# An indexer moved from split products on the whole array to plain float32 products on quarters of its rows

## The chip, the cores and the metric

The kernel runs on one core of a Trainium2 chip. The metric is device time in microseconds (us), the median of the timed runs. TensorE's granted clock stands at its upper level, 2.4 GHz, in every slice of the profile.

## What is computed

The reference is a trunk of two layers over 256 tokens of 1024 channels. Each layer projects the normed input to queries, keys and values of two attentions and to the inputs of a small "indexer"; the indexer's scores choose, for each query, the 64 keys that the first attention may look at. Then come both attentions, an output product and a gated feed-forward block. The change touches the indexer alone:

```python
iq = apply_rope(iq.reshape(b_, s_len, IDX_HEADS, IDX_DIM), cos_i, sin_i)   # 8 heads of 32
ik = apply_rope(ik[:, :, None, :], cos_i, sin_i)[:, :, 0, :]               # one key of 32
...
dots = jnp.einsum('bqhd,bsd->bqhs', iqb, ik, preferred_element_type=jnp.float32) * (IDX_DIM ** -0.5)
w = iwb.astype(jnp.float32) * (IDX_HEADS ** -0.5)
score = jnp.einsum('bqhs,bqh->bqs', jax.nn.relu(dots), w)
score = jnp.where(admissible[None], score, -jnp.inf)
_, idx = lax.top_k(score, topk)
```

## The kernel before, in words

The 256 tokens are two blocks (b = 0, 1) of 128, one per partition. All weights stream once from HBM in chunks of about 1 MB (`load`, L157). Each chunk is split in two halves: ScalarE casts it to `whi` (type float32r) at L174, VectorE writes the rest, `wlo`, at L175. A large product is then three matmuls, hi·hi, lo·hi and hi·lo (`mm3`, L193 to L198), each 512 columns wide as a rule. The main stream of TensorE takes the projections of a layer in the order idx, qb, kb, vb, qa, ka, va, then the output product (`wo`), gate and up (`ps_gate`, `ps_up`) and down (`dn`).

Between the large products stand small ones, as "threads": transposes, the indexer's products (`dots`), the logits (`lg_b`, `lg_a`) and so on. The class `Weave` sets TensorE's order when the program is built: a thread yields an estimated delay or names of events, `W.spend` adds an estimated cost to a running clock, and a thread goes on as soon as that clock has passed its due time. `DIX` is the delay between an indexer projection and its transposes, `DG` that between groups of two heads of the indexer. So TensorE's order is fixed by hand; ScalarE and VectorE are ordered by the framework's scheduler. Each engine executes its list in order, and a waiting instruction holds up all that stand behind it.

The indexer, for a block: the projection lands in `ps_idx`; `rope_evac` (L365) copies it to SBUF and rotates it, and L390 adds the two parts to `ixt`, nine vectors of 32 per token (eight queries, one key). L392 to L398 split these in hi and lo and lay them side by side, (hi, lo, hi, lo) for a query and (hi, hi, lo, lo) for the key, so that one head fills all 128 rows of the array and a single matmul of type float32r does all four products. L404 to L411 transpose the nine 128x128 squares (`ptx`, L202) and copy them to `iqT` and `ikT`. In `indexer` (L435) the eight heads come in four groups of two: two matmuls (L446) into one PSUM bank, a relu by ScalarE (L448), and two multiply-adds by VectorE (L451) into `score`. After that VectorE searches the 64 largest.

There are eight PSUM banks. A projection holds two of them while it accumulates; each `ptx`, `ptq` (transposes of the other queries and keys) and each group of `dots` takes one and gives it back when ScalarE has read it. `relu` has two buffers.

A plain float32 matmul of the program shows as two records in the trace, each with its own weight load; a float32r matmul and a transpose show as one.

Of the kernel before, what the change touches and what calls it, by code (L numbers as in the profile page):

```python
# [8 lines left out]
F32 = mybir.dt.float32  # L9
# [8 lines left out]
P = 128  # L18
# [14 lines left out]
LOWP = 100  # L33
DG = 2.0
DUP = 2.5
# [6 lines left out]
DROPE = 8.0  # L42
DIX = 13.0
DB = (8.0, 10.0)
# [4 lines left out]
class Weave:  # L49
    """Orders the tensor engine's work: one main stream of large products, and threads of small  # L50
    ones, each of which says how long (in estimated microseconds) its operands take to be ready."""

# [56 lines left out]
def tile_hybrid_trunk(ctx, tc, x, w_in, w_out, vecs, w_gate, w_up, w_down, g_final, rope, out):  # L109
# [5 lines left out]
    def bank(name):  # L115
        return psum.tile([P, 512], F32, tag="bank", bufs=8, name=name)
# [3 lines left out]

    # ---------------------------------------------------------------- weight stream
    NSUB = 1024
# [78 lines left out]
    def transpose(o, i):  # L201
        nc.tensor.transpose(o, i, ident)  # L202
        W.spend(0.107)

    # ---------------------------------------------------------------- inputs that stay
    LAMROW = 2 * DEPTH * KT + DEPTH
# [28 lines left out]

    # gains and lambda vectors, one per column
    gT = pool.tile([P, ROWS], F32, tag="gT", name="gT")
# [57 lines left out]
    def split_psum(pt, name, scales=None, tag="act", bufs=12):  # L295
        """Columns of a bank as hi and lo tiles; scales: one factor per partition for each of them."""
        n = pt.shape[1]
# [49 lines left out]
    def norm(kind, L, b, h):  # L347
        """One half of the transposes of x, scaled by the gain (the row factor is applied to the products)."""
        yield DN, ()
        norm_T(kind, L, b, h)  # L350
        norm_split(kind, L, b, h)
        if h == 1:
            rstd[kind, L, b] = norm_rstd(b, f"{kind}{L}{b}")

    # ---------------------------------------------------------------- what follows a projection
    T = {}

    def matT(t, o, name):
        """[tokens, 512] -> [128, 4, tokens], float32."""
        pt = bank(f"ptq_{name}").rearrange("p (k t) -> p k t", k=4)  # L360
        for k in range(4):
            transpose(pt[:, k], t[:, k * P:(k + 1) * P])
        nc.scalar.copy(o, pt)
# [17 lines left out]
    def after_proj(L, nm, b, ps):  # L381
        name = f"{nm}{L}{b}"
        r = rstd["mix", L, b]
        if nm == "idx":
# [3 lines left out]
            a, c = rope_evac(ps, r, b, 9, 32, name)  # L388
            t = pool.tile([P, 9, 32], F32, tag="hff", bufs=3, name=f"ixt{L}{b}")
            nc.vector.tensor_tensor(t.rearrange("p h d -> p (h d)"), a[:, :288], c[:, :288], op=ALU.add)  # L390
            # hi and lo side by side: (hi, lo, hi, lo) of a query meets (hi, hi, lo, lo) of a key
            sq = pool.tile([P, 8, 4, 32], F32R, tag=("kbT", "kaT")[b], bufs=1, name=f"ixq{L}{b}")  # L392
            sk = pool.tile([P, 1, 4, 32], F32R, tag="ixk", bufs=2, name=f"ixk{L}{b}")
            for st, hd, first, second in ((sq, slice(0, 8), slice(0, 4, 2), slice(1, 4, 2)),
                                          (sk, slice(8, 9), slice(0, 2), slice(2, 4))):
                src = t[:, hd].unsqueeze(2).to_broadcast([P, hd.stop - hd.start, 2, 32])
                nc.scalar.copy(st[:, :, first], src)
                nc.vector.tensor_tensor(st[:, :, second], src, st[:, :, first].bitcast(F32), op=ALU.subtract)  # L398
            yield DIX, ()
            iq = pool.tile([P, 8, P], F32R, tag="iqT", bufs=2, name=f"iqT{L}{b}")  # L400
            if b == 0:
                T["ik"] = pool.tile([P, S], F32R, tag="ikT", bufs=1, name=f"ikT{L}")
            flat = [v.bitcast(F32).rearrange("p h r d -> p h (r d)") for v in (sq, sk)]
            for g in range(2):  # L404
                pt = bank(f"ptx{L}{b}{g}").rearrange("p (k t) -> p k t", k=4)
                for k in range(4):
                    transpose(pt[:, k], flat[0][:, 4 * g + k])
                nc.scalar.copy(iq[:, 4 * g:4 * g + 4], pt)
            pt = bank(f"ptx{L}{b}2")
            transpose(pt[:, :P], flat[1][:, 0])  # L410
            nc.scalar.copy(T["ik"][:, b * P:(b + 1) * P], pt[:, :P])  # L411
            T["iq", b] = iq
        elif nm in ("va", "vb"):
# [15 lines left out]

    # ---------------------------------------------------------------- attention  # L430
    def small_mm(cost, *a, **k):
        nc.tensor.matmul(*a, **k)  # L432
        W.spend(cost)

    def indexer(L):  # L435
        for b in range(NB):
            yield 0, tuple(("idx", L, i) for i in range(b + 1))
            nk = (b + 1) * P
            sc = pool.tile([P, S], F32, tag="score", bufs=2, name=f"score{L}{b}")
            first = True  # L440
            for g in range(4):
                if g:
                    yield DG, ()
                ps = bank(f"dots{L}{b}{g}").rearrange("p (i k) -> p i k", i=2)
                for i in range(2):
                    small_mm(0.109, ps[:, i, :nk], T["iq", b][:, 2 * g + i], T["ik"][:, :nk], start=True, stop=True)  # L446
                rl = pool.tile([P, 2, S], F32, tag="relu", bufs=2, name=f"relu{L}{b}{g}")
                nc.scalar.activation(rl[:, :, :nk], ps[:, :, :nk], AF.Relu, scale=32 ** -0.5)  # L448
                for i in range(2):
                    h = 2 * g + i  # L450
                    nc.vector.scalar_tensor_tensor(sc[:, :nk], rl[:, i, :nk], T["iw", b][:, h:h + 1],  # L451
                                                   smask[:, b, :nk] if first else sc[:, :nk],
                                                   op0=ALU.mult, op1=ALU.add)
                    first = False
# [12 lines left out]
    def softmax_pair(L, b, q, k, mask, pair, name):  # L467
        """Unnormalized probabilities of two heads of one row group, and one over their sums."""
        nk = (b + 1) * P
# [120 lines left out]

    # ---------------------------------------------------------------- the feed-forward block
    ffT = {}
# [15 lines left out]

    # ---------------------------------------------------------------- the main stream
    def group(kind, L, key, n, first, after):  # L610
        """act @ w for both blocks; first: the acts are only being made, so one block after the other."""
        banks = [bank(f"ps_{key[1]}{L}{key[2] if len(key) > 2 else ''}{b}") for b in range(NB)]
# [95 lines left out]
    def final(b, cuts, gfin):  # L708
        """The last norm of one block, piece by piece as its columns come."""
        n = len(cuts)  # L710
# [28 lines left out]
    def startup(after):  # L739
        n = NCOL["idx"]  # L740
        with tc.manual_schedule(engines={ENG.Activation, ENG.DVE}):
# [15 lines left out]

            # the first block in plain float32, which waits for no splitting
            first = [begin(0, h) for h in range(2)]
# [85 lines left out]
```

## Time and profile before

| | us |
|---|---|
| median of 3 runs | 647.33 (646.92 to 649.78) |
| profiled execution, span from first to last instruction | 645.0 |
| TensorE busy | 635.2 (98% of the span) |
| VectorE busy | 437.9 (68%) |
| ScalarE busy | 365.2 (57%) |

The profiled execution is known by its span alone; it lies 2.3 us under the median of the runs. Busy time of TensorE is that of its matmul records, whose ends are modelled, so a small wait can hide in it; the distance between the starts of two records tells more. An engine's idle time matters only where TensorE waits for it.

### The profile page before, as it was taken

Reading aid. Unit: us, or ns where it says so; the run is one execution under the profiler, and the core shown is the slowest. Engines: PE = TensorE matmul, PEld = TensorE weight load, DVE = VectorE, ACT = ScalarE, POOL = GpSimd, SP = SyncE. Lnnn points to the kernel's source line nnn. Section 1 sums busy time; section 2 is a strip of 40 time slices with the busy share of each in tenths; the row PEclk is TensorE's granted clock in tenths of the full one; section 3 lists DMA queues with packets and bytes.
Section 4 is the critical chain, followed back from the end, with each engine's and each line's share of the span. In section 5 each row is a group of like instructions: output and inputs, shape, how many; then the busy total and the mean of one; then the engine's idle time right before and its main releaser. Section 6 shows DMA issues by size and latency. Waiting matters only on the chain.

```text
span 645.0 us, 8819 instructions
## 1 busy us (share of the span) xinstructions
PE 635.2 (98%) x3256; PEld 526.5 (82%) x3256; DVE 437.9 (68%) x922; ACT 365.2 (57%) x636; POOL 1.9 (0%) x12
## 2 busy tenths in 40 slices
PE   8999999999999999999999999999999999999995
PEld 5888787888888889888898888778888888898885
DVE  6899997596456555544598999866765455464445
ACT  7868586675544454333487678765744554443322
POOL 1000000000000000000000000000000000000000
PEclk9999999999999999999999999999999999999999
DMA  9773453326555655555276533323655555555501
GB/s 317 228 227 101 133 187 136 131 90 236 188 168 170 197 193 196 175 191 162 69 262 203 188 131 132 132 65 131 215 180 193 195 196 166 197 163 193 196 34 65
DMA packets 49907, 108.59 MB, mean 168 GB/s; under 512 B 1826, under 2 KB 8520, under 8 KB 49864
## 3 DMA queue, kind: packets, MB, share of 16 engines
q1 hardware_dynamic: 49392, 106.96, 49.6%
q10 hardware_dynamic: 472, 1.07, 0.5%
q8 instruction: 25, 0.41, 0.3%
q14 instruction: 18, 0.15, 0.1%
HBM read 106.97 MB, written 1.05 MB: 167 GB/s over the span
## 4 chain that ended last, share of the span: by engine, by line
PE 97%; DMA 1%; DVE 0%; SPq 0%; ACT 0%; issue 0%; ACTq 0%
PE ps_gate L196 6%; PE ps_gate L198 6%; PE dn L196 6%; PE dn L197 6%; PE dn L198 6%; PE ps_gate L197 6%; PE ps_up L198 6%; PE ps_up L196 6%; PE ps_up L197 6%; PE wo L198 2%; PE wo L196 2%; PE wo L197 2%; PE lg_a L432 2%; PE pth L202 1%; PE ps_va L196 1%; PE ps_vb L196 1%
## 5 line engine op out<-in xcount | busy, mean ns | idle before, releaser
L175 DVE TENSOR_TENSOR wlo<-wraw,whi 128x1024 fp32r<-128x1024 f32 (+1 forms) x204 | 244.5, 1205 | 141.9 <-ACT whi L174 138.4
L174 ACT CAST whi<-wraw 128x1024 fp32r<-128x1024 f32 (+1 forms) x204 | 209.6, 1040 | 150.8 <-PE dn L197 50.0
L196 PE MATMUL ps_gate<-whi,hi_ffn 128*128 128x512 f32 (+1 forms) x192 | 73.7, 384 | 0.0
L196 PE MATMUL dn<-whi,hi_ff 128*128 128x512 f32 (+1 forms) x198 | 73.2, 370 | 0.0
L197 PE MATMUL dn<-whi,lo_ff 128*128 128x512 f32 (+1 forms) x198 | 72.7, 367 | 0.0
L198 PE MATMUL dn<-wlo,hi_ff 128*128 128x512 f32 (+1 forms) x198 | 72.5, 366 | 0.0
L198 PE MATMUL ps_gate<-wlo,hi_ffn 128*128 128x512 f32 (+1 forms) x192 | 71.7, 373 | 0.0
L198 PE MATMUL ps_up<-wlo,hi_ffn 128*128 128x512 f32 (+1 forms) x192 | 71.4, 372 | 0.0
L197 PE MATMUL ps_up<-whi,lo_ffn 128*128 128x512 f32 (+1 forms) x192 | 71.4, 372 | 0.0
L196 PE MATMUL ps_up<-whi,hi_ffn 128*128 128x512 f32 (+1 forms) x192 | 71.4, 372 | 0.0
L197 PE MATMUL ps_gate<-whi,lo_ffn 128*128 128x512 f32 (+1 forms) x192 | 71.4, 372 | 0.0
L198 PEld LDWEIGHTS dn<-wlo,hi_ff 128*128 128x128 f32 x198 | 37.3, 188 | 6.2
L196 PEld LDWEIGHTS dn<-whi,hi_ff 128*128 128x128 f32 x198 | 37.4, 189 | 5.9
L197 PEld LDWEIGHTS dn<-whi,lo_ff 128*128 128x128 f32 x198 | 37.4, 189 | 5.8
L198 PEld LDWEIGHTS ps_gate<-wlo,hi_ffn 128*128 128x128 f32 x192 | 36.1, 188 | 6.6
L197 PEld LDWEIGHTS ps_up<-whi,lo_ffn 128*128 128x128 f32 x192 | 36.2, 189 | 6.2
L198 PEld LDWEIGHTS ps_up<-wlo,hi_ffn 128*128 128x128 f32 x192 | 36.2, 188 | 6.2
L196 PEld LDWEIGHTS ps_up<-whi,hi_ffn 128*128 128x128 f32 x192 | 36.2, 189 | 6.2
L197 PEld LDWEIGHTS ps_gate<-whi,lo_ffn 128*128 128x128 f32 x192 | 36.3, 189 | 5.7
L196 PEld LDWEIGHTS ps_gate<-whi,hi_ffn 128*128 128x128 f32 x192 | 36.2, 189 | 5.5
L303 ACT CAST hi_ff<-pth 128x512 fp32r<-128x512 f32 (+1 forms) x24 | 13.1, 544 | 20.0 <-PE pth L202 20.0
L304 DVE TENSOR_TENSOR lo_ff<-pth,hi_ff 128x512 fp32r<-128x512 f32 (+1 forms) x24 | 15.5, 645 | 8.9 <-ACT hi_ff L303 8.9
(320 smaller groups left out, 1060.8 us busy)
## 6 DMA issues: line engine op xcount, KB each, us to landing
wraw<-in_w_in_dram SPq DMA_DIRECT2D x24, 1024.0 KB, 5.1
wraw<-in_w_gate_dram SPq DMA_DIRECT2D x22, 1024.0 KB, 5.1
wraw<-in_w_up_dram SPq DMA_DIRECT2D x22, 1024.0 KB, 5.2
wraw<-in_w_down_dram SPq DMA_DIRECT2D x22, 1024.0 KB, 4.9
wraw<-in_w_out_dram SPq DMA_DIRECT2D x8, 1024.0 KB, 5.0
wraw<-in_w_in_dram SPq DMA_DIRECT2D x4, 296.0 KB, 5.0
wraw<-in_w_in_dram SPq DMA_DIRECT2D x2, 592.0 KB, 3.9
x<-in_x_dram SPq DMA_DIRECT2D x2, 256.0 KB, 3.1
```

The costliest lines, as they stand in the source:

```text
L174: nc.scalar.copy(hi, raw[c][:, s:s + step])
L175: nc.vector.tensor_tensor(lo, raw[c][:, s:s + step], hi.bitcast(F32), op=ALU.subtract)
L196: nc.tensor.matmul(ps, hi, whi, start=first, stop=False)
L197: nc.tensor.matmul(ps, lo, whi, start=False, stop=False)
L198: nc.tensor.matmul(ps, hi, wlo, start=False, stop=last)
L202: nc.tensor.transpose(o, i, ident)
L303: nc.scalar.copy(hi[:, :n], pt)
L304: nc.vector.tensor_tensor(lo[:, :n], pt, hi[:, :n].bitcast(F32), op=ALU.subtract)
L432: nc.tensor.matmul(*a, **k)
```

## The change

The indexer's vectors are no longer split. `ixt` gets twelve vectors of 32: eight queries and the key four times. Three transposes per block (four vectors each) take the place of nine: two of queries, one of the repeated key, all into one bank. After them, head 4·i + g has its 32 numbers on partitions 32·g to 32·g + 31, and so does a copy of the key. Each matmul contracts over 32 rows, in plain float32, and heads g = 0 to 3 stand on different quarters of the array's rows. The eight matmuls of a block are issued together, into four banks that are taken at once; head order in a bank is (g, 4 + g). The relus and multiply-adds stay eight and sixteen in number per layer and keep their sizes. `DG` is gone, `DIX` falls from 13 to 10. The order in which the heads' products are added changes. Comments and docstrings are removed too.

```diff
-DIX = 13.0
+DIX = 10.0
...
-            t = pool.tile([P, 9, 32], F32, tag="hff", bufs=3, name=f"ixt{L}{b}")
-            nc.vector.tensor_tensor(t.rearrange("p h d -> p (h d)"), a[:, :288], c[:, :288], op=ALU.add)
...
-            sq = pool.tile([P, 8, 4, 32], F32R, tag=("kbT", "kaT")[b], bufs=1, name=f"ixq{L}{b}")
-            sk = pool.tile([P, 1, 4, 32], F32R, tag="ixk", bufs=2, name=f"ixk{L}{b}")
-            for st, hd, first, second in ((sq, slice(0, 8), slice(0, 4, 2), slice(1, 4, 2)),
-                                          (sk, slice(8, 9), slice(0, 2), slice(2, 4))):
-                src = t[:, hd].unsqueeze(2).to_broadcast([P, hd.stop - hd.start, 2, 32])
-                nc.scalar.copy(st[:, :, first], src)
-                nc.vector.tensor_tensor(st[:, :, second], src, st[:, :, first].bitcast(F32), op=ALU.subtract)
+            t = pool.tile([P, 12, 32], F32, tag="hff", bufs=3, name=f"ixt{L}{b}")
+            keys = [v[:, 256:288].unsqueeze(1).to_broadcast([P, 4, 32]) for v in (a, c)]
+            nc.vector.tensor_tensor(t[:, :8].rearrange("p h d -> p (h d)"), a[:, :256], c[:, :256], op=ALU.add)
+            nc.vector.tensor_tensor(t[:, 8:], keys[0], keys[1], op=ALU.add)
             yield DIX, ()
-            iq = pool.tile([P, 8, P], F32R, tag="iqT", bufs=2, name=f"iqT{L}{b}")
+
+            pt = bank(f"ptx{L}{b}").rearrange("p (k t) -> p k t", k=4)
+            for k in range(3):
+                transpose(pt[:, k], t[:, 4 * k:4 * k + 4].rearrange("p h d -> p (h d)"))
+            iq = T["iq", b] = pool.tile([P, 2, P], F32, tag="iqT", bufs=2, name=f"iqT{L}{b}")
             if b == 0:
-                T["ik"] = pool.tile([P, S], F32R, tag="ikT", bufs=1, name=f"ikT{L}")
-            flat = [v.bitcast(F32).rearrange("p h r d -> p h (r d)") for v in (sq, sk)]
-            for g in range(2):
-                pt = bank(f"ptx{L}{b}{g}").rearrange("p (k t) -> p k t", k=4)
-                for k in range(4):
-                    transpose(pt[:, k], flat[0][:, 4 * g + k])
-                nc.scalar.copy(iq[:, 4 * g:4 * g + 4], pt)
-            pt = bank(f"ptx{L}{b}2")
-            transpose(pt[:, :P], flat[1][:, 0])
-            nc.scalar.copy(T["ik"][:, b * P:(b + 1) * P], pt[:, :P])
-            T["iq", b] = iq
+                T["ik"] = pool.tile([P, S], F32, tag="ikT", bufs=1, name=f"ikT{L}")
+            nc.scalar.copy(T["ik"][:, b * P:(b + 1) * P], pt[:, 2])
+            nc.scalar.copy(iq, pt[:, :2])
...
+            banks = [bank(f"dots{L}{b}{g}").rearrange("p (i k) -> p i k", i=2) for g in range(4)]
+            for i in range(2):
+                for g in range(4):
+                    rws = slice(32 * g, 32 * g + 32)
+                    small_mm(0.054 * (b + 1), banks[g][:, i, :nk], T["iq", b][rws, i], T["ik"][rws, :nk],
+                             start=True, stop=True)
             first = True
             for g in range(4):
-                if g:
-                    yield DG, ()
-                ps = bank(f"dots{L}{b}{g}").rearrange("p (i k) -> p i k", i=2)
+                rl = pool.tile([P, 2, S], F32, tag="relu", bufs=2, name=f"relu{L}{b}{g}")
+                nc.scalar.activation(rl[:, :, :nk], banks[g][:, :, :nk], AF.Relu, scale=32 ** -0.5)
                 for i in range(2):
-                    small_mm(0.109, ps[:, i, :nk], T["iq", b][:, 2 * g + i], T["ik"][:, :nk], start=True, stop=True)
...
-                    h = 2 * g + i
+                    h = 4 * i + g
```

**TensorE's order, first layer, before.** The rows begin in the projection kb (`ps_kb`); `ptx` are the indexer's transposes, `ptq_qb` those of qb, and `dots` of 128 columns belong to block 0.

```order
L196 MATMUL ps_kb_372<-whi_0_332,hi_mix_175 128x512
L197 MATMUL ps_kb_372<-whi_0_332,lo_mix_176 128x512
L198 MATMUL ps_kb_372<-wlo_0_333,hi_mix_175 128x512
L202 MATMUL ptx_407<-ident,ixq_284 128x128 x4
L202 MATMUL ptx_413<-ident,ixq_284 128x128 x4
L202 MATMUL ptx_419<-ident,ixk_285 128x128
L202 MATMUL ptx_423<-ident,ixq_300 128x128 x4
L202 MATMUL ptx_429<-ident,ixq_300 128x128 x4
L202 MATMUL ptx_435<-ident,ixk_301 128x128
...
L202 MATMUL ptq_qb_442<-ident,rp_qb_354 128x128 x4
L432 MATMUL dots_449<-ikT_406,iqT_405 128x128 x2
```

**The same place after the change**, with what each instruction waits for. `ps_qb` is the projection ahead of kb; `dots` of 256 columns belong to block 1.

```order
L201 MATMUL ptx_373<-ident,ixt_282 128x128 [waits DVE_49]
...
L197 MATMUL ps_kb_361<-wlo_2_327,hi_mix_123 128x512
L421 MATMUL dots_405<-ikT_378,iqT_377 128x128 [waits Activation_49]
L421 MATMUL dots_406<-ikT_378,iqT_377 128x128 [waits PE_49]
L421 MATMUL dots_407<-ikT_378,iqT_377 128x128 [waits PE_49]
L421 MATMUL dots_408<-ikT_378,iqT_377 128x128
...
L421 MATMUL dots_468<-ikT_378,iqT_385 128x256 [waits Activation_49]
L421 MATMUL dots_469<-ikT_378,iqT_385 128x256 [waits PE_49]
L421 MATMUL dots_470<-ikT_378,iqT_385 128x256 [waits PE_49]
L421 MATMUL dots_471<-ikT_378,iqT_385 128x256 [waits Activation_49]
L421 MATMUL dots_468<-ikT_378,iqT_385 128x256
```

The six transposes now stand right behind qb, ahead of all of kb; nine matmuls of kb follow, and then all sixteen `dots` of both blocks without a break, where eight visits of two stood between kb and vb. `dots_471`, the fourth bank of block 1, is the same bank as `dots_405`, the first of block 0, so it waits for ScalarE's relu of that. In the second layer the order has three transposes, nine large matmuls and eight `dots` for block 0, and the same again for block 1.

**ScalarE's order at that place, before**: copies of the transposes (`iqT`, `ikT`), casts of weights (`whi`), and the first relu.

```order
L408 CAST iqT_405<-ptx_407 128x512
L408 CAST iqT_405<-ptx_413 128x512
L411 CAST ikT_406<-ptx_419 128x128
L408 CAST iqT_422<-ptx_423 128x512
L408 CAST iqT_422<-ptx_429 128x512
L411 CAST ikT_406<-ptx_435 128x128
L174 CAST whi_0_541<-wraw_373 128x1024
L363 COPY qb00T<-ptq_qb_442 128x512
L448 ACTIVATE relu_452<-dots_449 128x2x128
```

And after:

```order
L173 CAST whi_0_554<-wraw_320 128x1024
L369 ACTIVATE rp_qb_388<-ps_qb_269,rs_mix0y_255 128x512
L400 COPY ikT_378<-ptx_373 128x128
L401 COPY iqT_377<-ptx_373 128x256
L400 COPY ikT_378<-ptx_381 128x128
L401 COPY iqT_385<-ptx_381 128x256
L173 CAST whi_2_558<-wraw_320 128x1024
L438 ACTIVATE relu_417<-dots_405 128x2x128
L438 ACTIVATE relu_421<-dots_406 128x2x128
L438 ACTIVATE relu_425<-dots_407 128x2x128
```

Six copies became four smaller ones, and a cast of weights, `whi_2_558`, stands between them and the first relu.

## Rows read from the trace of the kernel before

**Rows 1.** The page: busy time of TensorE, its granted clock, and the chain.
```profile
PE 635.2 (98%) x3256; PEld 526.5 (82%) x3256; DVE 437.9 (68%) x922; ACT 365.2 (57%) x636; POOL 1.9 (0%) x12
...
PEclk9999999999999999999999999999999999999999
...
PE 97%; DMA 1%; DVE 0%; SPq 0%; ACT 0%; issue 0%; ACTq 0%
```

**Rows 2.** TensorE's timeline, layer 0: start us, length us, line, operation, tiles, shape, count.
```profile
27.10 0.39 PE L196 MATMUL ps_kb<-whi,hi_mix 128*128 128x512 f32 x1
...
30.50 1.03 PE L202 MATMUL ptx<-ident,ixq 128*128 128x128 f32 x8
31.37 0.27 PE L202 MATMUL ptx<-ident,ixk 128*128 128x128 f32 x1
31.48 1.04 PE L202 MATMUL ptx<-ident,ixq 128*128 128x128 f32 x8
```

**Rows 3.** The same view: four of the indexer's products, two of each block.
```profile
42.84 0.62 PE L432 MATMUL dots<-ikT,iqT 128*128 128x128 f32 x4
43.30 0.40 PE L196 MATMUL ps_vb<-whi,hi_mix 128*128 128x512 f32 x1
```

**Rows 4.** The same view: logits of two pairs of heads, on both halves of the rows.
```profile
53.78 0.39 PE L198 MATMUL ps_vb<-wlo,hi_mix 128*128 128x512 f32 x1
54.10 0.72 PE L432 MATMUL lg_b<-kbT,qb00T 64*128 64x128 f32 x8
54.75 0.50 PE L196 MATMUL ps_vb<-whi,hi_mix 128*128 128x512 f32 x1
55.09 0.39 PE L197 MATMUL ps_vb<-whi,lo_mix 128*128 128x512 f32 x1
```

**Rows 5.** The same view: logits of one pair of heads, on one half of the rows.
```profile
93.55 0.71 PE L432 MATMUL lg_a<-kaT,qa00T 64*128 64x128 f32 x4
94.19 0.50 PE L196 MATMUL ps_va<-whi,hi_mix 128*128 128x512 f32 x1
```

**Rows 6.** The same view: logits of block 1, 256 columns, on both halves.
```profile
68.32 0.39 PE L198 MATMUL ps_qa<-wlo,hi_mix 128*128 128x512 f32 x1
68.64 1.14 PE L432 MATMUL lg_b<-kbT,qb01T 64*128 64x256 f32 x8
69.71 0.44 PE L202 MATMUL ppt_b<-ident,p_b 128*128 128x128 f32 x2
```

**Rows 7.** ScalarE's timeline, layer 0; in brackets the idle time before, and its releaser.
```profile
27.58 1.06 ACT L174 CAST whi<-wraw 128x1024 fp32r<-128x1024 f32 x1 [1.45 <-DMA wraw<-in_w_in_dram]
28.54 0.61 ACT L397 CAST ixq<-ixt 128x512 fp32r<-128x512 f32 x1
...
29.20 0.68 ACT L370 ACTIVATE rp_qb<-ps_qb,rs_mix0y 128x512 f32<-128x512 f32 x1
29.79 1.04 ACT L174 CAST whi<-wraw 128x1024 fp32r<-128x1024 f32 x1
...
32.09 0.29 ACT L411 CAST ikT<-ptx 128x128 fp32r<-128x128 f32 x1
32.25 1.11 ACT L408 CAST iqT<-ptx 128x512 fp32r<-128x512 f32 x2
...
34.78 0.46 ACT L448 ACTIVATE relu<-dots 128x256 f32<-128x256 f32 x1
```

**Rows 8.** VectorE's timeline, layer 0; last, of one tile: count, ns min/median/max.
```profile
25.61 1.22 DVE L175 TENSOR_TENSOR wlo<-wraw,whi 128x1024 fp32r<-128x1024 f32 x1
26.75 0.69 DVE L398 TENSOR_TENSOR ixq<-ixt,ixq 128x512 fp32r<-128x512 f32 x1
...
27.85 0.69 DVE L374 TENSOR_TENSOR rp_qb<-rp_qb,rope_sb 128x512 f32<-128x512 f32 x1
28.46 0.69 DVE L377 TENSOR_TENSOR rp_qb<-rp_qb,rope_sb 128x512 f32<-128x512 f32 x1
...
L451 DVE SCALAR_TENSOR_TENSOR score<-relu,iw,score x28: 347/416/491, 38.3 to 367.0; 128x128 f32<-128x128 f32 x14, 128x256 f32<-128x256 f32 x14
```

More of the change, by code (lines that the diff above doesn't have):

```diff
@@ L33 @@
 LOWP = 100
-DG = 2.0
 DUP = 2.5
@@ L439, in indexer @@
             sc = pool.tile([P, S], F32, tag="score", bufs=2, name=f"score{L}{b}")
+            banks = [bank(f"dots{L}{b}{g}").rearrange("p (i k) -> p i k", i=2) for g in range(4)]
[4 more added lines that the diff above has]
+                             start=True, stop=True)
             first = True
             for g in range(4):
-                if g:
-                    yield DG, ()
-                ps = bank(f"dots{L}{b}{g}").rearrange("p (i k) -> p i k", i=2)
+                rl = pool.tile([P, 2, S], F32, tag="relu", bufs=2, name=f"relu{L}{b}{g}")
+                nc.scalar.activation(rl[:, :, :nk], banks[g][:, :, :nk], AF.Relu, scale=32 ** -0.5)
                 for i in range(2):
-                    small_mm(0.109, ps[:, i, :nk], T["iq", b][:, 2 * g + i], T["ik"][:, :nk], start=True, stop=True)
-                rl = pool.tile([P, 2, S], F32, tag="relu", bufs=2, name=f"relu{L}{b}{g}")
-                nc.scalar.activation(rl[:, :, :nk], ps[:, :, :nk], AF.Relu, scale=32 ** -0.5)
-                for i in range(2):
-                    h = 2 * g + i
+                    h = 4 * i + g
                     nc.vector.scalar_tensor_tensor(sc[:, :nk], rl[:, i, :nk], T["iw", b][:, h:h + 1],
```

## The prediction

> **What bounds the kernel now.** I read the page first: TensorE is busy 98% of the span, its granted clock is at the top digit in all forty slices, and the chain that ended last is 97% TensorE [rows 1]. So a matmul record that goes saves its own time, and work that goes from ScalarE or VectorE saves nothing until TensorE waits for it. Then I read TensorE's timeline at the indexer, looking at distances between starts, since the lengths overlap: fifteen large matmuls of 512 columns lie between 27.10 and 30.50, 0.227 us each [rows 2]. Last I read the two engines that feed the indexer there, for what will be late when TensorE needs less time [rows 7, 8].
>
> **Transposes.** Nine `ptx` go from 30.50 to 31.48 [rows 2], 0.109 us each. Two layers of two blocks had 36 and keep 12: 24 x 0.109 = **2.61 us gained**, all on the path.
>
> **The products before.** Four `dots` take 42.84 to 43.30, 0.46 us, with both widths among them and no loss at either edge [rows 3]. There are 32, so 8 x 0.46 = 3.68 us.
>
> **The products after.** No row shows a float32 product on a quarter of the rows; the nearest are the logits, plain float32 on a half. One pair of heads on one half, four records in a chain, takes 93.55 to 94.19, 0.64 us [rows 5]. Two pairs, one on each half, eight records, take 54.10 to 54.75, 0.65 us [rows 4]: the second half runs beside the first for 0.01 us. Such a visit has a price of its own. From the last large matmul before it to the second one behind it pass 1.31 us (53.78 to 55.09 [rows 4]), where two large matmuls take 0.45: the visit costs 0.86. With 256 columns the records take 68.64 to 69.71, 1.07 us [rows 6], 0.42 more than with 128: 0.86 + 0.42 = 1.28. Of this about 0.43 is entering and leaving, and the rest four records at 0.107 (128 columns) or 0.21 (256).
>
> In the changed kernel a quarter holds two heads of a block, hence again four records in a chain. If four quarters overlap as two halves do, block 0 costs 0.86 and block 1 costs 1.28. Layer 1 pays both, 2.14. Layer 0 issues all sixteen in one visit and enters once: 2.14 - 0.43 = 1.71. Sum 3.85 against 3.68: **0.17 us lost**. From below, the price is at least 0.86 a visit, also for the wide ones: 3 x 0.86 = 2.58, a gain of 1.1. From above, no record overlaps another: that is the third rival, +7.7 us. I take the value by the halves, because it is the same instruction on the same array with two partners instead of four.
>
> **What goes elsewhere.** ScalarE loses the casts at L397, VectorE the subtractions at L398, and the copies at L408 become smaller. I cost this at nothing, in either direction: TensorE's large matmuls cover it. The transposes now come earlier, right behind qb, at 27.1. Their operand for block 1 is ready about 27.5: the `wlo` that starts at 25.61 gives way at 26.75 [rows 8] and starts 0.2 later for the second add, then come two adds. TensorE has three transposes of block 0 to do until 27.4, so under 0.1 us is lost.
>
> **The wait that the change adds.** Without `DG`, layer 0 issues sixteen products at once, which want eight banks while kb holds one. The order shows the result: the fourth bank of block 1 is the first of block 0 and waits for its relu, and four products stand behind it. I walk this by rows. TensorE: qb ends at 27.10, six transposes to 27.76, nine large matmuls to 29.8, entry, first round at 29.9; block 0 takes until 30.5, where the fourth bank would be wanted. ScalarE: the cast that waited for its weights starts at 27.58 and gives way at 28.54 [rows 7]; qb's copy 0.59 (29.20 to 29.79), to 29.13; two copies of 128 columns at 0.16 (32.09 to 32.25) and two of 256 at about 0.27 (between 0.16 and the half of 1.11 that one with 512 columns takes), to 29.97; the cast `whi_2_558`, 0.96, to 30.93; the relu about 0.42, to 31.35 [rows 7]. So the fourth bank is free at 31.4 and not at 30.5: **0.9 us lost**, since the rounds of the other three quarters that run meanwhile have to be repeated for the rest. It is bounded by nothing below (the cast stands behind the relu) and by about two casts above, 1.9.
>
> Behind it: the third relu waits until VectorE has read the first one twice (two buffers), and the transposes `ptq_qb` wait for the bank that this relu frees. VectorE comes to the first score at about 32.7, behind the rotation of qb (0.60 apiece, 27.85 to 28.46 [rows 8]) and two `wlo`; the second score stands behind another addition and ends, at 0.347 (the least of its group, 128 columns [rows 8]), about 34.0; the relu ends at 34.4. TensorE arrives at 34.35 or so: **0.1 us lost**. The later relus alternate with two `wlo` of 1.14, and the next `ptq_qb`, twelve large matmuls on, needs its bank at 37.6, some 0.5 us after the relu by the same walk. Layer 1 has nine large matmuls between transposes and products in each block, 2 us, and puts three transposes and nine more between the two blocks: all its banks are free by then, and I see no wait.
>
> **The sum.** -2.61 + 0.17 + 0.9 + 0.1 = -1.4 us. The profiled span of 645.0 becomes 643.6; against the median of 647.33, which lies 2.3 above that span, **645.9 us**. That is 0.2%: no change that a measurement of this kernel can tell, whose bound I put at 0.5%, 3.2 us.
>
> **Rivals.**
>
> *No wait at all (644.9).* If the scheduler's cast gives way, or its weights come earlier, the 1.0 us of waits go. For it: the cast depends on a landing, and the idle time ahead of it (1.45 us in rows 7) is the DMA's. Against it: the order is fixed when the program is built, with that cast ahead of the relu. Chance 0.12.
>
> *The heads start in strict order (649.0).* A head has two records on the same quarter, so the second must follow the first; if no record may start before those ahead of it in the list, eight heads need nine rounds instead of four. Five more rounds of 0.107 and of 0.21 are 1.6 us a layer, 3.2 us in all: 645.9 + 3.2 = 649.1, less a shared round 649.0, slower than before by 1.7. Against it speak the logits: in their list the four records of one half stand ahead of all of the other, and in strict order would need seven rounds, but the visit is 0.65 us long, four [rows 4]. The Trainium skill's page "TensorE: Matmul & The Clock Gate", in "Part 3: Packing small matmuls — row/col tiling", says of packed matmuls that they start and end in strict program order, without reordering. By that rule the forecast would be this rival's; rows 4 against rows 5 do not agree with it for halves, and no row shows quarters. Chance 0.12.
>
> *The quarters do not overlap (653.6, slower).* One mechanism in one place: the array serves one group of 32 rows at a time. Then eight heads are sixteen rounds, twelve more than the four: 12 x 0.107 + 12 x 0.21 = 3.8 us a layer, 7.7 in all, +1.0% over before. It would be slower by over 0.5% from 4.7 us over the forecast, that is from seven of the twelve. For it: no row shows more than two groups side by side. Against it: the second half cost 0.01 us [rows 4, 5]. Chance 0.06.
>
> *The waits grow (648.0).* VectorE falls one or two `wlo` behind (1.14 each), relus and banks follow, and both `ptq_qb` of layer 0 wait: about 2 us more. Against it: 0.5 us of room at the second one. Chance 0.08.
>
> **How the numbers follow.** The forecast has 0.62. The range runs from 644.0, where neither wait nor price of the visits shows and the runs fall on their lower side (lowest run 0.4 under the median), to 649.1, which takes in strict order and grown waits; the quarters without overlap stay out, and so do tails of 0.1 together. Slower by over 0.5% (over 650.6): the third rival and a little of the others, 0.08. Faster by over 0.5% (under 644.1) would need more than all of the transposes: 0.08, for prices I may have missed and for scatter. No change: 0.84.
>
> **What would show it.** In the profile after: twelve `ptx` records at 0.109; `dots` as 64 records, starting in fours some 10 ns apart, in rounds of 0.107 and 0.21; about 0.43 us lost at the edges of each visit; in layer 0 a gap of 0.9 us in the visit, released by a relu, and none in layer 1. Wrong would be: single files of `dots` records, eight or sixteen rounds, or gaps over 0.5 us at `ptq_qb` or at kb's second bank.

## The result, and the profile after

The changed kernel takes **656.21 us** (655.69 to 657.43, 4 runs); the kernel before, run beside it, 647.35. The ratio is 1.0136, 95% interval 1.0121 to 1.0151: slower by 1.4%, 8.9 us. The forecast was 645.9, range 644.0 to 649.1, with a chance of 0.08 for slower. It was wrong.

The page of the profile after, lines that answer to [rows 1]:

```profile
span 653.9 us, 8817 instructions
...
PE 638.1 (98%) x3264; PEld 524.3 (80%) x3264; DVE 437.9 (67%) x918; ACT 358.9 (55%) x624; POOL 1.9 (0%) x12
...
PEclk9999899999999999999999999999999999999998
...
PE 85%; DVE 10%; ACT 2%; issue 1%; DMA 0%; ACTq 0%; DVEq 0%
```

TensorE's share of the chain that ended last fell from 97% to 85%, and VectorE, which had none of it, has 10%. The span is no longer TensorE's alone. The granted clock, at the top digit in all slices before, shows an 8 in the fifth (65 to 82 us) and in the last.

What the change set out to do is there. TensorE's timeline at the transposes and products of layer 0 and at the products of layer 1 (start us, length us, line, operation, tiles, shape, count), beside [rows 2 to 4]:

```profile
27.00 0.82 PE L201 MATMUL ptx<-ident,ixt 128*128 128x128 f32 x6
27.58 0.48 PE L195 MATMUL ps_kb<-whi,hi_mix 128*128 128x512 f32 x1
...
29.51 0.39 PE L197 MATMUL ps_kb<-wlo,hi_mix 128*128 128x512 f32 x1
29.83 2.31 PE L421 MATMUL dots<-ikT,iqT 32*128 32x128 f32 x32
32.06 0.50 PE L195 MATMUL ps_kb<-whi,hi_mix 128*128 128x512 f32 x1
32.40 0.40 PE L196 MATMUL ps_kb<-whi,lo_mix 128*128 128x512 f32 x1
...
346.60 0.39 PE L197 MATMUL ps_qb<-wlo,hi_mix 128*128 128x512 f32 x1
346.92 0.73 PE L421 MATMUL dots<-ikT,iqT 32*128 32x128 f32 x16
347.58 0.50 PE L195 MATMUL ps_qb<-whi,hi_mix 128*128 128x512 f32 x1
347.91 0.40 PE L196 MATMUL ps_qb<-whi,lo_mix 128*128 128x512 f32 x1
```

The sixteen records of layer 1's block 0 take 0.66 us (346.92 to 347.58): four rounds of four. From the last large matmul ahead to the second behind pass 1.31 us; less two large ones, 0.45, the visit costs 0.86, as forecast. Layer 0's visit lasts from 29.51 to 32.40, 2.44 us net.

The time went elsewhere. attn_b is the second attention. It works through four items (a block and half of its heads), each of two pairs of heads: logits (`lg_b`), a softmax that begins with a reduction on VectorE, the probabilities `p_b`, and their transposes `ppt_b`. attn_a is the first attention, which needs the search's mask. The same view where `ppt_b` begins, in layer 0 and layer 1; in brackets the idle time and its releaser:

```profile
61.34 0.39 PE L197 MATMUL ps_qa<-wlo,hi_mix 128*128 128x512 f32 x1
65.48 0.33 PE L201 MATMUL ppt_b<-ident,p_b 128*128 128x128 f32 x1 [3.76 <-DVE p_b L501]
66.07 0.48 PE L201 MATMUL ppt_b<-ident,p_b 128*128 128x128 f32 x1 [0.26 <-DVE p_b L501]
66.20 0.78 PE L195 MATMUL ps_qa<-whi,hi_mix 128*128 128x512 f32 x1
...
68.48 0.63 PE L197 MATMUL ps_qa<-wlo,hi_mix 128*128 128x512 f32 x1
...
384.68 0.59 PE L201 MATMUL ppt_b<-ident,p_b 128*128 128x128 f32 x2 [2.13 <-DVE p_b L501]
385.03 0.48 PE L195 MATMUL ps_qa<-whi,hi_mix 128*128 128x512 f32 x1
```

Before, layer 0's `ppt_b` followed without a wait:

```profile
60.10 0.39 PE L198 MATMUL ps_qa<-wlo,hi_mix 128*128 128x512 f32 x1
60.33 0.38 PE L202 MATMUL ppt_b<-ident,p_b 128*128 128x128 f32 x2
```

After, TensorE stands still for 3.76 and 2.13 us, and the releaser is VectorE's L501, which makes the probabilities that are to be transposed. A table by stretches of TensorE's busy time and granted clock tells what follows the first wait (start:end us, length, busy with records, clock, DMA share, GB/s):

```profile
61.00:65.40 4.40, 0.72 (x4) 1.00 0.23 36
...
66.20:68.90 2.70, 2.70 (x7) 0.50 0.58 222
```

In these 2.7 us the clock is at half, 1.2 of 2.4 GHz: large matmuls start 0.43 us apart instead of 0.23, which costs half of the 2.7, 1.3 us. (The clock stands at half for 3.4 us in all, from 65.7 to 69.1.) Behind layer 1's shorter wait it stays at the top.

Now VectorE, which is late. Its timeline in layer 0 from the search for the 64 largest (L449 finds eight, L451 strikes them out) to the first results of attn_b, after:

```profile
54.09 0.29 DVE L449 MAX8 m<-topk 128x8 f32<-128x128 f32 x1
...
54.49 0.28 DVE L451 MATCH_REPLACE8 topk<-m,topk 128x128 f32<-128x128 f32 x1
54.80 0.29 DVE L449 MAX8 m<-topk 128x8 f32<-128x128 f32 x1
...
55.73 0.41 DVE L449 MAX8 m<-score 128x8 f32<-128x256 f32 x1
...
56.38 0.41 DVE L451 MATCH_REPLACE8 topk<-m,score 128x256 f32<-128x256 f32 x1
...
57.18 0.27 DVE L469 CUSTOM_DVE_ANT_0 p_b<-lg_b,smask 128x128 f32<-128x128 f32 x1
...
65.68 0.33 DVE L501 SCALAR_TENSOR_TENSOR p_b<-p_b,rc_b,p_b 128x128 f32<-128x128 f32 x1
```

The same place before (its L479 is L469 after, L511 is L501):

```profile
51.30 1.22 DVE L175 TENSOR_TENSOR wlo<-wraw,whi 128x1024 fp32r<-128x1024 f32 x1
52.43 0.49 DVE L451 SCALAR_TENSOR_TENSOR score<-relu,iw,score 128x256 f32<-128x256 f32 x1
52.82 0.29 DVE L479 CUSTOM_DVE_ANT_0 p_b<-lg_b,smask 128x128 f32<-128x128 f32 x1
...
57.72 0.33 DVE L511 SCALAR_TENSOR_TENSOR p_b<-p_b,rc_b,p_b 128x128 f32<-128x128 f32 x1
```

Before, scores were still being added up when attn_b's first softmax reduction (L479) came. After, the scores are done early, and the search takes the place in between: the reduction starts at 57.18 instead of 52.82, and the second L501 at 65.68 instead of 57.72, 8 us late. Counted along VectorE's order, 2 rounds of the search stood ahead of the first reduction in layer 0 and 1 in layer 1; now 9 and 12. Up to the second L501 it is 5 then and 15 now. A round occupies VectorE for 0.48 us with 128 columns and for 0.74 with 256 (by starts in such a timeline); the ten more are three of the one and seven of the other, 6.6 us. Two more subtractions of weights, 1.14 us each, stand there too; the four subtractions at L398, 1.5 us together, are gone. VectorE's work in all is the same (437.9 us on both pages). It is the order that moved.

From here on a wait without a row beside it is told as the distance between two starts over the usual one, which is 0.1 to 0.3 us more than the idle time in a row's brackets. Taken together: 3.92 + 0.48 us at layer 0's `ppt_b`, 1.3 of slow clock, 2.44 at layer 1's `ppt_b`, 0.77 at its `ptq_kb`, and 0.50 and 0.45 at attn_a's first logits: 9.9 us. The time rose by 8.9, so the rest of the change, the forecast's own terms, gave back 1.0.

### The profile page after: what moved, and what is told of

It reads as the page before. It is cut to its first block, busy times and chain, and to the rows that moved or that the text cites. A ratio compares the mean times of both kernels' runs of the same rounds, so it can differ in the third digit from the quotient of the medians.

```text
span 653.9 us, 8817 instructions
## 1 busy us (share of the span) xinstructions
PE 638.1 (98%) x3264; PEld 524.3 (80%) x3264; DVE 437.9 (67%) x918; ACT 358.9 (55%) x624; POOL 1.9 (0%) x12
## 3 DMA queue, kind: packets, MB, share of 16 engines
q10 hardware_dynamic: 472, 1.07, 0.5%
## 4 chain that ended last, share of the span: by engine, by line
PE 85%; DVE 10%; ACT 2%; issue 1%; DMA 0%; ACTq 0%; DVEq 0%
PE dn L195 6%; PE ps_gate L197 6%; PE ps_gate L195 6%; PE dn L197 6%; PE dn L196 6%; PE ps_gate L196 6%; PE ps_up L196 6%; PE ps_up L197 6%; PE ps_up L195 6%; DVE wlo L174 4%; PE wo L195 2%; PE wo L197 2%; PE wo L196 2%; PE lg_a L421 2%; PE pth L201 1%
## 5 line engine op out<-in xcount | busy, mean ns | idle before, releaser
L472 ACT ACTIVATE p_b<-p_b,mx_b 128x128 f32<-128x128 f32 (+1 forms) x32 | 14.4, 454 | 17.9 <-DVE mx_b L469 17.6
```

What stands on the lines that cost most here:

```text
L472: nc.scalar.activation(p[:, i, :nk], p[:, i, :nk], AF.Exp, scale=-1.0, bias=mx[:, i:i + 1], accum_out=sm[:, i:i + 1])
```

## The experiments

Two theories stood against each other at first: that the search's place in VectorE's order makes the waits, and that the quarters, the four banks or the earlier transposes have a price that the rows hide. From e5 on there was a third: that VectorE is too full for any order.

**e1, the search held back.** A multiply-add of one column makes the search read `nl` of attn_b's second item:

```diff
+            yield 0, (("gate", L),)
             with tc.high_priority(offset=-LOWP):
+                g = T["gate", L]
+                nc.vector.scalar_tensor_tensor(sc[:, :1], g[:, :1], 0.0, sc[:, :1], op0=ALU.mult, op1=ALU.add)
                 cur = sc
```

> The changed kernel with one true dependence added: the search for the 64 largest (all its rounds, both blocks of a layer) starts only when the softmax of the first two items of the second attention has been normalised; one multiply-add on one column of score per block carries it. Nothing is left out. Theory A (VectorE's fixed order: the search stands ahead of the softmax, and TensorE waits at the first transposes of probabilities): the gaps of 3.9 and 2.3 us there go, the fall of the granted clock behind the first with them, span about 643, time about 645, faster than before by some 2 us. Theory B (the products on quarters, the four banks at once or the earlier transposes cost the time): the search has no part in it, so the time stays near 656.

Measured 655.74 us, ratio 1.0121 (1.0105 to 1.0137): the time that the rival named, and not mine of 645. The waits at 61 and 382 us are gone, but they came back at later items. TensorE's timeline:

```profile
60.62 0.38 PE L201 MATMUL ppt_b<-ident,p_b 128*128 128x128 f32 x2
...
93.07 0.41 PE L201 MATMUL ppt_b<-ident,p_b 128*128 128x128 f32 x2 [0.75 <-DVE p_b L504]
95.11 0.55 PE L201 MATMUL ppt_b<-ident,p_b 128*128 128x128 f32 x2 [1.63 <-DVE p_b L504]
```

Behind the last of these the granted clock falls to half for 3.4 us, from 95.3 on. So the search does make the first wait, but held back as a whole it makes others. The time alone would have pointed at the rival. The edit was also less clean than meant: the gate stands in the loop over blocks, so block 1's products waited with it (they start at 55.28 us).

**e2, the same gate in the kernel before.**

> The kernel before with the same dependence, as a control. Theory A: in the kernel before two rounds of the search stood ahead of the first softmax and TensorE hardly waited, so there is nothing to gain: 647.3 within 0.7. Theory B says nothing else. If it were faster by 2 us, the gate by itself would be the gain, and not the transposes.

The edit is that of e1, block 1's products held back included. Measured 659.36, ratio 1.0181 (1.0165 to 1.0197): a miss. With a late search the old kernel loses 11.8 us; its longest idle time (2.44 us) is ahead of a `ppt_b` of layer 1. Neither quarters nor fewer transposes are needed to lose such an amount.

**e3, the kernel before without its pacing** (`DG = 0.0`, nothing else).

> The kernel before with DG set to 0 and nothing else: split products on the whole array, nine transposes per block, DIX 13; only the groups of two heads come together. The built order has five rounds of the search ahead of the first softmax of layer 0 (two before, nine in the changed kernel) and ten in layer 1 (one before, twelve changed). Theory A: the same wait at the same place, smaller in layer 0, near 2 us in layer 1; 649 to 655. Theory B: as fast as before, 647.3 within 0.7, since neither quarters nor four banks are in it.

Measured 655.63, ratio 1.012 (1.0102 to 1.0137). Without the pauses between pairs of products the scores are done earlier and 5 and 10 rounds stand ahead of the first reduction. The waits are 2.43 us at layer 0's `ptq_qb`, whose releaser is a relu, 1.14 at a `ppt_b` and 1.65 at attn_a's logits. My expectation failed in place, and by a little in time (it ended at 655): layer 0's `ppt_b` waits nowhere for over 0.4 us, and the longest wait is at the transposes of qb. But the pacing alone, which the change dropped as well, is worth 8 us in the kernel before.

**e4, the search cut** from eight rounds to one in the changed kernel. It leaves out seven rounds, so that attn_a's mask keeps 8 keys of a query instead of 64.

```diff
-                for it in range(TOPK // 8):
+                for it in range(1):
```

> The changed kernel with one round of the search in place of eight; the other seven are left out. Theory A: with 14 fewer search steps per block VectorE is at the softmax in time; gaps at the first transposes of probabilities under 0.5 us each, time about 645. Theory B: 656, as no part of the products changes.

Measured 647.8, ratio 1.0006 (0.9996 to 1.0015). All waits at `ppt_b` are gone. What stays are 0.44 and 0.45 us at attn_a's first logits, which wait for ScalarE's copy of ka's transposes, and 0.8 in layer 0's products, whose visit costs 2.53 us. The time is 2.8 us over the 645 that I had expected. The search is the cause of the waits at `ppt_b`; how much of it is the load and how much the order this run does not tell.

**e5 to e8, scores and search later**, by a number in the indexer: e5 to e7 raise `DIX`, the pause ahead of the transposes, from 10 to 20, 24 and 28; e8 leaves it and adds a pause ahead of each block's products.

```diff
-DIX = 10.0
+DIX = 20.0
...
+            yield 12.0, ()
             sc = pool.tile([P, S], F32, tag="score", bufs=2, name=f"score{L}{b}")
```

> The changed kernel with one number changed: the indexer's transposes wait an estimated 20 us for their operand instead of 10, and so the products, the scores and the search come later. In VectorE's order 4 rounds of the search then stand ahead of the first softmax reduction of attn_b in either layer, instead of 9 and 12. Theory (the place of the search in VectorE's order sets the wait): the gaps ahead of ppt_b of 3.9 and 2.3 us shrink to under 0.5 each, the clock does not fall, time 646 to 648. Rival (the quarters or the transposes themselves cost it): 655 to 657. Second rival (VectorE is full, and whatever the search is moved behind, it makes some other wait): 650 to 655 with gaps at other places.

> The same number at 24: 3 rounds ahead of the first softmax reduction in layer 0, 6 in layer 1. Theory: layer 0 as with 20; in layer 1 six rounds at 0.6 to 0.7 us are half of the twelve of the changed kernel, whose wait was 2.3, and the eight that made no wait with the search cut in number were two: a gap of 0 to 0.7 there, time 646 to 649. Rivals as with 20: 655 to 657, or 650 to 655.

> The same number at 28: no round of the search stands ahead of the first four softmax reductions of either layer, and eight rounds stand between the last of the second item and the first of the third. That is nearly the order of the changed kernel with the search held back by a gate, which waited ahead of the third item's ppt_b and took 655.7. Theory of the search's place: too late is as bad as too early, 652 to 656, with gaps over 1 us at ppt_b of the third and fourth item. Rival (only rounds ahead of the first item count): 645 to 647.

> The changed kernel with its transposes as early as they are, and each block's products held back by an estimated 12 us more. Rounds ahead of the first softmax reduction: 1 in layer 0, 3 in layer 1, nearly the 2 and 1 of the kernel before, and the next ones also spread as there. Theory: no gap over 0.5 us ahead of any ppt_b, 645 to 647.5, no worse than before. Rival (the quarters or the transposes cost it): 655 to 657. Rival (VectorE is full): 650 to 655.

| run | rounds ahead of the first reduction, layer 0, 1 | us | ratio |
|---|---|---|---|
| e5, 20 | 4, 4 | 652.40 | 1.0068 (1.0051 to 1.0085) |
| e6, 24 | 3, 6 | 656.12 | 1.0123 (1.0105 to 1.0141) |
| e7, 28 | 0, 0 | 652.08 | 1.0069 (1.0053 to 1.0085) |
| e8, products 12 | 1, 3 | 652.79 | 1.0078 (1.0063 to 1.0094) |

My expectation held for e7, and for its time alone (its waits are many and small, none over 0.8 us); it failed for the other three. The times hold more than waits: the granted clock falls to half for 3.4 us twice in e5 and e6 and once in e7 and e8 (in e7 from 55.1 on). TensorE's timeline shows where each waits longest, in e5 ahead of attn_b's first logits of layer 0:

```profile
52.57 0.85 PE L421 MATMUL lg_b<-kbT,qb00T 64*128 64x128 f32 x8 [2.33 <-ACT kbT L362]
```

In e6 ahead of the same logits of layer 1:

```profile
372.73 1.23 PE L421 MATMUL lg_b<-kbT,qb10T 64*128 64x128 f32 x8 [3.22 <-ACT kbT L362]
```

In e8 ahead of the transposes of attn_b's last item in layer 0:

```profile
93.45 0.99 PE L201 MATMUL ppt_b<-ident,p_b 128*128 128x128 f32 x4 [2.60 <-DVE p_b L502]
```

In e5 the copy of kb's transposes stands behind relus on ScalarE, and these wait for VectorE, because a relu's buffer is free only when two scores have read it. ScalarE's timeline of e5:

```profile
50.50 0.60 ACT L438 ACTIVATE relu<-dots 128x512 f32<-128x512 f32 x1 [0.65 <-DVE score L441]
50.99 1.04 ACT L173 CAST whi<-wraw 128x1024 fp32r<-128x1024 f32 x1
51.93 0.59 ACT L362 COPY kbT<-ptq_kb 128x512 f32<-128x512 f32 x1
```

So a count at the first reduction is not enough: later scores now collide with kb, as an earlier search did with attn_b. Four shifts of one number only chose which piece of work was late. That spoke for the second rival, a VectorE too full for any order.

**e9, the search pinned to its old places.** To separate order from load, everything of the change stays, the search becomes a thread of its own, and single rounds wait, as in e1, for the reduction behind which they stood before:

```diff
+            W.spawn(search(L, b, sc))
...
+        for it in range(TOPK // 8):
+            if (L, b, it) in GATES:
+                ev = (L,) + GATES[L, b, it]
+                yield 0, (("sm",) + ev,)
+                with tc.high_priority(offset=-LOWP):
+                    nc.vector.scalar_tensor_tensor(cur[:, :1], T[("mx",) + ev][:, :1], 0.0, cur[:, :1],
+                                                   op0=ALU.mult, op1=ALU.add)
```

> The changed kernel, products and transposes untouched, with its search held to nearly the places that it had in the kernel before: a round waits, through a multiply-add of one column, for the softmax reduction behind which it stood there. Rounds ahead of the first reductions of the eight pairs of attn_b: layer 0 2, 3, 5, 5, 12, 12, 15, 15 (before 2, 3, 5, 6, 13, 14, 16, 16), layer 1 1, 4, 5, 6, 11, 12, 14, 15 (before 1, 5, 7, 8, 13, 15, 16, 16); the weights' subtractions keep the counts of the changed kernel. Theory (the search's place is the cause): no gap over 0.5 us ahead of any ppt_b, 645.5 to 648. Rival (VectorE is full, any order of this program's work waits somewhere): 651 to 655, gaps at other tiles. Rival (quarters, banks or transposes cost it): 655 to 657.

Measured **648.41**, ratio 1.0013 (1.0004 to 1.0022): 7.8 us less than the changed kernel, a little over the span that I had given. VectorE's timeline of e9 at the first softmax reduction, the gate (L457) and the search behind it:

```profile
53.98 0.28 DVE L483 CUSTOM_DVE_ANT_0 p_b<-lg_b,smask 128x128 f32<-128x128 f32 x1
...
54.39 0.15 DVE L457 SCALAR_TENSOR_TENSOR topk<-mx_b,topk 128x1 f32<-128x1 f32 x1
54.58 0.29 DVE L461 MAX8 m<-topk 128x8 f32<-128x128 f32 x1
```

And TensorE's at the place of the 3.76 us, with no wait:

```profile
62.43 0.39 PE L197 MATMUL ps_qa<-wlo,hi_mix 128*128 128x512 f32 x1
62.66 0.38 PE L201 MATMUL ppt_b<-ident,p_b 128*128 128x128 f32 x2
```

This is the run that settles it. Quarters, transposes, banks and VectorE's load are those of the changed kernel, with thirteen small gates more. The edit also lets attn_a's logits wait for the mask when TensorE's order is made, but that order came out unchanged: in both traces TensorE's 3264 records follow each other alike. The counts of weights' subtractions ahead of attn_b's reductions differ by one at most. What the edit moves is the search. The scheduler then placed other work anew around it, some 30 of ScalarE's 624 instructions and some 50 of VectorE's 818 outside the search; no run separates their share. The ratio's interval leaves 0.04 to 0.22% over the kernel before; two waits at attn_a's logits, named under e12, stand in that rest.

**e10, held at two points a layer only.** Edit: the table of gates of e9 cut to four entries.

> As the pinned kernel, but with two gates a layer only: the third round (layer 1: second) waits for the second pair of the first item, and the other block's first round for the last pair of the second item. Rounds ahead of the pairs: layer 0 2, 2, 4, 4, 11, 12, 16, 16, layer 1 1, 1, 2, 2, 9, 10, 14, 16. Theory: as pinned or 1 us more, since from 4 to 11 rounds are bunched behind the second item and may be late for the third: 645.5 to 650. Rivals: 651 to 655, and 655 to 657.

Measured 650.17, ratio 1.0039 (1.0026 to 1.0051). Waits of 1.5 and 1.2 us at attn_a's first logits and one of 0.47 at a `ppt_b` of layer 1: of the pins' 7.8 us some three quarters come with two coarse gates a layer (656.2 to 650.2 is 6.0), the rest with the finer ones.

**e11, the pinned kernel with VectorE relieved:** one of two multiplications of each rotation on GpSimd.

```diff
-        nc.vector.tensor_tensor(c[:, :n].rearrange("p (h t d) -> p h t d", h=nh, t=2),
+        (nc.vector if nh == 9 else nc.gpsimd).tensor_tensor(c[:, :n].rearrange("p (h t d) -> p h t d", h=nh, t=2),
```

> The pinned kernel with VectorE relieved: one of the two multiplications of each rotation of qb, kb, qa and ka (16 in all, about 0.6 us each) goes to GpSimd, which does nothing in this stretch. If VectorE's load rather than the order alone is what waits, this takes what is left of the waits: 644 to 646, faster than the pinned kernel by up to 2 us. Rival: GpSimd needs several us for one, or slows VectorE beside it, and the rotations come late: slower than the pinned kernel by 1 to 6 us, with gaps ahead of ptq tiles.

Measured 662.4, ratio 1.0226 (1.0211 to 1.0241): slower than the pinned kernel by 14 us, more than twice the worst I had given. The groups of GpSimd (count, busy us and mean ns):

```profile
L376 POOL TENSOR_TENSOR rp_qb<-rp_qb,rope_sb 128x512 f32<-128x512 f32 x4 | 9.1, 2276 | 279.5 <-ACT rp_qb L369 249.7 <-DVE ixt L391 24.4 <-issue 5.4
...
L376 POOL TENSOR_TENSOR rp_kb<-rp_kb,rope_sb 128x512 f32<-128x512 f32 x4 | 5.8, 1445 | 24.1 <-ACT rp_kb L369 24.1
```

One takes 1.4 to 2.3 us there, against 0.69 on VectorE [rows 8]. The page "GPSIMD Engine Reference" of the Trainium skill, section "3.1 Elementwise — side-by-side cycle accounting", puts an addition of two float32 tiles at about twice VectorE's time; here it is 2.1 to 3.3 times. TensorE waits 3.35 us at layer 0's `ptq_qb` and 2.98 at layer 1's first logits of attn_a. How much of the 14 us is GpSimd's slowness and how much the order that the scheduler made around it was not separated.

**e12, the pinned kernel without its last wait.** In e9 attn_a's first logits wait 0.89 us in layer 0 and 0.82 in layer 1, for ScalarE's copy of ka's transposes.

```diff
-        W.done((nm, L, b), DT)
+        W.done((nm, L, b), DT + (1.2 if nm == "ka" else 0.0))
```

> The pinned kernel with one estimate raised: the copy of ka's transposes is taken to be ready 1.2 us later, so that the first logits of attn_a stand six large matmuls further back in TensorE's order, behind the second ptq_ka. In the pinned kernel they wait 0.89 us in layer 0 and 0.82 in layer 1 for that copy. Theory (with the search in its place, waits of this size are all that is left, and the TensorE time that the change saves then shows): those two gaps go, 648.4 becomes 646.5 to 647.0, level with the kernel before or up to 0.2% faster. Rival (something that no gap shows takes the rest): no change against the pinned kernel, 648 to 648.5.

Measured **646.94** (11 runs), beside 647.32 before (15 runs); ratio 0.9991 (0.9982 to 1.0001). Both waits are gone; the logits stand behind the second `ptq_ka`:

```profile
93.47 0.63 PE L201 MATMUL ptq_ka<-ident,rp_ka 128*128 128x128 f32 x4
94.03 0.71 PE L421 MATMUL lg_a<-kaT,qa00T 64*128 64x128 f32 x4
```

Its page's chain is 94% TensorE and 1% VectorE. Between the first matmul of qb and the first of the feed-forward block pass 120.38 us in layer 0 (before 120.55) and 119.18 in layer 1 (before 119.97): together 1.0 us less. The time lies in the span that I had given. Against the kernel before the interval just reaches no change, so I call it level, not faster.

## Why the prediction was wrong

**Transposes: right.** Six take 0.58 us (27.00 to 27.58), and three in layer 1 0.25. All twelve take 1.07 us by starts where 36 took 3.68: 2.6 us gained.

**Products: right, to the hundredth where nothing waits.** Layer 1's visits cost 0.86 and 1.29 us, forecast 0.86 and 1.28. Taking the price from the logits on halves was sound: four quarters overlap as two halves do.

**The wait in layer 0's products: right in place, a little less in size.** The visit costs 2.44 us where 1.71 without a wait was forecast, so the wait is 0.73 and not 0.9; the first relu, which frees the bank, starts at 30.57 and not at 30.93. The same visit costs 2.49 us in e9 and 2.68 in e12, waits of 0.78 and 0.97, so the size varies from kernel to kernel about the forecast. `ptq_qb` starts at 34.24 without a wait (forecast 0.1).

**The rivals on TensorE fell.** There are four rounds a block, not nine and not sixteen. Four rounds in the 0.66 us of layer 1's block 0 do not agree with the strict order that the Trainium skill's page "TensorE: Matmul & The Clock Gate", "Part 3: Packing small matmuls — row/col tiling", gives packed matmuls, if a head's two records, which share a quarter, stand next to each other in the list, as the rival took it: the records start in fours. No view shows the list record by record, so where the second records stand in it is not shown. (The third rival's twelve more rounds of each width come to 7.6 us in two layers, not 7.7; nothing hangs on it.)

**The step that failed is "What goes elsewhere … I cost this at nothing, in either direction: TensorE's large matmuls cover it."** I walked ScalarE and VectorE to layer 0's `ptq_qb` and stopped; of layer 1 I wrote "I see no wait", and there TensorE stood still for 2.13 us. The cover holds while what VectorE does next is not wanted soon. But layer 0's products, spread from 33.5 to 51.5 us before, now lie between 29.8 and 32.1, the scores follow them, and the search, which has a low priority and was put wherever the order had room, moved forward behind them. The diff does not touch it, and it landed ahead of attn_b's softmax. So 6.6 us of search became 3.8 us of wait in layer 0, and the granted clock fell to half behind that wait for 3.4 us. e9 shows it: with the search back at nearly its old places the kernel is 0.8 us slower than before, and not 8.9.

The rival "the waits grow" had the engine right, and the place, the size and the work wrong: it let VectorE fall one or two `wlo` behind at `ptq_qb`, for 2 us. It could have been seen: in the kernel before VectorE is busy for 29.67 of the 30 us from 40 to 70, with no wait of TensorE, so its order there had little room; and its new order could be counted before any run.

**What is left of the gain.** With the search pinned and the logits moved, e12 takes 646.9 against the forecast of 645.9: of the 1.4 us forecast, 0.4 shows in the medians, which the interval does not tell from nothing, and 1.0 between the marks of the traces. Part of the missing rest is in TensorE's order outside the indexer: the eight transposes `pt_mb` of a layer take 1.02 us in e12 (1.00 in the changed kernel) and 0.71 before, by distances between starts; they stand among other neighbours now. The rest stays open.

## What to carry to other kernels

When a change makes a producer earlier, follow its consumers on every in-order engine down to the next thing the bottleneck waits for, low-priority work above all: list what stands ahead of each due instruction before and after, and price the difference. An engine that is nearly always busy and never waited for, as VectorE was here, leaves little room for a new order. Moving one number that shifts everything (e5 to e8) traded one wait for another, while pinning the one moved piece to its old places (e9) both showed the cause and mended most of it. And work taken off the bottleneck is worth only what the order of the other engines lets through: here 2.6 us of transposes became at best 0.4, with the search and attn_a's logits moved as well.

## What the runs showed of the hardware that I had not expected

- Four float32 matmuls on four quarters of the rows start 7 ns apart (29.826, 29.833, 29.840 and 29.846 us in the single records of the first round), in rounds of 0.11 us with 128 columns and 0.21 with 256; the first round of a visit takes 0.1 longer. Eight heads on four quarters take 0.66 us, where four heads on two halves took 0.65 [rows 4]: three partners cost as little as one.
- The granted clock fell to half, for 3.4 us, behind an idle time of 3.76 us (changed kernel, layer 0) and behind one of 2.26 (e3, matmuls 0.43 us apart from 40.25 on), but not behind one of 2.13 (changed kernel, layer 1). The length of that one wait does not decide it: the clock fell behind 1.60 us too (e5, at half from 370.5 to 373.9) and at 55.1 us in e7, where no idle time near by was over 0.61, and it stayed at the top behind 2.44 us (e2, layer 1) and 3.19 (e11, layer 0's `ptq_qb`). What decides it these runs do not show.
- A round of the search with 256 columns, in a row of its own, takes 0.98 us (375.30 to 376.28 in layer 1 of the changed kernel, from one strike-out to the next) where its three instructions occupy VectorE for 0.74 when other work stands between them: each reads what the one before wrote.
